# A decoder step on one core: the sample's requests ordered behind a power on POOL, a buffer of its own for the attention's queries, and the softmax factor of the cross-attention on ScalarE

## The chip, the cores and the metric

The kernel runs on one core of a Trainium2 chip. A core has TensorE (matmul; PE in the profile, with PEld for its weight loads), VectorE (DVE), ScalarE (ACT), GpSimd (POOL) and SyncE (SP). DMA requests are issued from queues: here SP asks for the weights and for most of the prompt's data, ACT for some stores, and POOL for everything large that the sample needs. Each of these engines works through its own list of instructions in order, so a request that waits for a free buffer holds up what stands behind it on the same engine. The metric is the time of one execution on the device in microseconds, here the median of several runs.

## The reference

One step of a decoder layer for two groups of rows that share the weights: a prompt of 1024 rows, and a sample of 8 requests with one new row each and 8192 cached positions behind it. Cut to what matters:

```python
# per group: x is (1, 1024, 1024) for the prompt and (8, 1, 1024) for the sample
q, k, v, logf, u, z = mixer_inputs(rmsnorm(x, g_mix), w_in, b_f, g_sgu_v)
att = fox_prompt(q, k, v, logf)          # causal, 8 heads of 64, with a forget term
#   or fox_sample(...)                   # against 64 pages of 128 cached keys and values per request
x = x + concat(rmsnorm(att), rmsnorm(sgu(u, z))) @ w_o
x = x + cross_attend(rmsnorm(x, g_cross), mk, mv, w_cq, w_co)   # 4 heads of 256, 256 memory rows
h = rmsnorm(x, g_ffn) @ w_up             # 2 x 2816 columns, then a causal convolution of width 3
x = x + (silu(gate) * val) @ w_down
y = rmsnorm(x, g_final)

def cross_attend(xn, mk, mv, w_cq, w_co):
    q = xn @ w_cq
    s = einsum('bqhd,bmhd->bhqm', q, mk) * 256 ** -0.5
    return einsum('bhqm,bmhd->bqhd', softmax(s), mv) @ w_co
```

Besides the two results, the new keys, values, forget terms, memory keys and values and the last rows of the convolution are returned.

## The kernel before

**Prompt.** Each large matmul is made of three: both operands are split into a rounded part and a rest (`split`: ScalarE writes the rounded part, VectorE the rest), and `gemm3` adds the three products that count. Weights come in pieces of 128 x 1024 through `wraw` and `wload` (L247, split at L233 and L234). The 1024 rows go through in two halves. `p1` makes the input projection; its last columns are done for four row tiles at once by `by_rows`. Then come `attention(0)`, `attention(1)`, and for each half the merge, the output projection, the cross-attention `cross`, and the gated MLP `ffn`.

**Attention.** It works on four pairs of heads. For each pair `load` fetches queries (L693), keys (L699) and values (L700), and `setup`, a generator of two steps, prepares the operands: the first step transposes the queries (L710) and splits them (L717, L734), the second does the same with the keys (L739, L744, L748). Then `scores` makes the maxima (L773, L776) and the exponentials (L774, L777), `turn` transposes them (L796) and `values` multiplies by the values (L812). The queries' tile comes from `T2`, a ring of seven buffers which also holds the exponentials of the first half, evictions on their way to memory (L680, for example) and other rows. The load and the first step of pair 0 are asked for inside `p1` by `early`, just before the last `by_rows`.

**Cross-attention.** For each head, `weigh` takes the row maxima of the raw scores, two row tiles at a time (L1137, VectorE), multiplies them by the factor of the row, `rq` (L1138, VectorE), and passes them as bias to the exponentials (L1141, ScalarE), which use `rq` as scale:

```python
nc.vector.tensor_reduce(mx[:, g2], sv, axis=AX.X, op=ALU.max, negate=True)
nc.vector.tensor_tensor(mx[:, g2], mx[:, g2], rq[:, g2], op=ALU.mult)
```

**Sample.** Its work is a background generator, `sample`, mixed into the prompt's at a pace given by hand (`PACE`). `decode` reads the cached keys and values of the 8 requests, 1 MB at a time, into four buffers (`KV`). VectorE multiplies and adds for the keys (L1384, L1388), PE for the values (L1444). Then `sample_rest` takes the 8 rows through the layer: `sample_proj` with `w_o`, a norm, `sample_proj` with `w_cq` (L1548 requests, L284 multiplies, L1538 adds up), the memory keys and values, `w_co`, a norm, `w_up` (L1700, L1709) and `w_down` (L1745, L1754). All these pages go through the same four buffers, and their requests stand on POOL. The norm `rms8` squares on ScalarE (L228), adds (L1520), and `rstd_of` scales (L221, VectorE) and raises to the power -1/2 on POOL (L222). The rows are then scaled (L1528) and transposed (L309). Between the second norm and `w_up`, the state of the convolution is read into one of the four buffers and a part of it stored again from there (L1691, to the output `o_s1`).

**Order.** The program is written in the order of these generators. A planner then lays out each engine's list when the program is built: of what could start, by its own estimate of durations, it takes what was written first. `tc.issue_after(ins)` orders the instructions of a block behind `ins` on the engine of `ins`; it adds no wait between engines.

Of the kernel before, what the change touches and what calls it, by code (L numbers as in the profile page):

```python
# [7 lines left out]
F32 = mybir.dt.float32  # L8
# [10 lines left out]
P = 128  # L19
D = 1024  # L20
# [58 lines left out]
def build(nc, tc, ctx, a, phases=None):  # L79
# [38 lines left out]
        return t  # L118

    def T2(n=512, dt=F32):  # L120
        return tpool.tile([P, 520], dt, tag="t2", bufs=NT, name=nm("t2"))[:, :n]

    def KV():
        return dpool.tile([P, 2048], F32, tag="kv", bufs=NKV, name=nm("kv"))
# [99 lines left out]

    def ssq_into(dst, src):
        n = src.shape[-1]
        j = tpool.tile([P, 1024], BF16, tag="junk", bufs=1, name=nm("junk"))[: src.shape[0], :n]
        nc.scalar.activation(j, src, AF.Square, accum_out=dst)  # L228

    def split(src, h, l, scale=None):  # L230
# [455 lines left out]
    def attention(hf, late=None, at=3):  # L686
# [2 lines left out]

        def load(hp):  # L690
            cs = slice(hp * P, (hp + 1) * P)
            qn = T2().rearrange("p (i c) -> p i c", c=P)
            nc.sync.dma_start(qn, q_d[hf * 512 : (hf + 1) * 512, cs].rearrange("(i p) c -> p i c", p=P))  # L693
            if hf == 0:
                kvn = U([P, 2 * nk, P])
                kn, vn = kvn[:, :nk, :], kvn[:, nk:, :]
            else:
                kn, vn = T2().rearrange("p (i c) -> p i c", c=P), U([P, nk, P])
            nc.sync.dma_start(kn, k_d[hf * 512 : nk * P, cs].rearrange("(i p) c -> p i c", p=P))  # L699
            nc.sync.dma_start(vn, v_d[: nk * P, cs].rearrange("(i p) c -> p i c", p=P))  # L700
            return qn, kn, vn
# [144 lines left out]

        got = []
        first = setup(0, *load(0))
        next(first)
        yield 2  # L850
        for _ in first:
            pass
        nxt = None
# [232 lines left out]
    def cross(xt, sq):  # L1086
# [37 lines left out]

        def weigh(h):
            mx = sm([P, 4], "cmx", 2)
            pp[h] = U([P, 4, 256])
            l4 = sm([P, 4], "cl", 2)
            r4 = sm([P, 4], "cr", 2)
            for g in range(2):  # L1130
                sv = BK().rearrange("p (i m) -> p i m", m=256)
                for i2 in range(2):
                    i = g * 2 + i2
                    for dd in range(2):
                        mmul(sv[:, i2, :], q2[h][:, dd, i * P : (i + 1) * P], mkT[h][:, dd, :], start=(dd == 0), stop=(dd == 1))
                g2 = slice(g * 2, g * 2 + 2)
                nc.vector.tensor_reduce(mx[:, g2], sv, axis=AX.X, op=ALU.max, negate=True)  # L1137
                nc.vector.tensor_tensor(mx[:, g2], mx[:, g2], rq[:, g2], op=ALU.mult)  # L1138
                for i2 in range(2):
                    i = g * 2 + i2  # L1140
                    nc.scalar.activation(  # L1141
                        pp[h][:, i, :], sv[:, i2, :], AF.Exp, bias=mx[:, i : i + 1], scale=rq[:, i : i + 1], accum_out=l4[:, i : i + 1]
                    )
            nc.vector.reciprocal(r4, l4)
            for i in range(4):
                nc.scalar.activation(pp[h][:, i, :], pp[h][:, i, :], AF.Copy, scale=r4[:, i : i + 1])
# [364 lines left out]
            yield left  # L1511


    def rms8(src):

        ss = sm([8, 2], "ss2", 1)
        for n in range(2):
            ssq_into(ss[:, n : n + 1], src[n])
        st = sm([8, 1], "sss", 1)
        nc.vector.tensor_tensor(st, ss[:, 0:1], ss[:, 1:2], op=ALU.add)  # L1520
        return rstd_of(st, D, 1, "r1")

    def sample_norm(src, gain, dst):
        r = rms8(src)
# [16 lines left out]
    def sample_proj(w, xT, fin):  # L1541
        outs = []
        for n in range(2):
            ps = (DV, MS)[n]()
            for kk in range(4):
                if kk % 2 == 0:
                    raw = KV().rearrange("p (k n) -> p k n", n=512)
                    nc.gpsimd.dma_start(raw, w[kk * 256 : (kk + 2) * 256, n * 512 : (n + 1) * 512].rearrange("(k p) n -> p k n", p=P))  # L1548
                    yield 1
                sample_mm(ps, raw[:, (kk % 2) * 2 : (kk % 2) * 2 + 2, :], kk, xT, 512)  # L1550
            outs.append(sample_out(n, ps, fin))
            next(outs[n])
        for o in outs:
            yield from o
        yield 1

    def sample_rest(xs):
# [46 lines left out]
        for b in range(8):  # L1604
            qb = [D2(), D2()]
            for n in range(2):
                nc.gpsimd.dma_start(qb[n], q2s_d[b : b + 1, n * 512 : (n + 1) * 512].broadcast_to((P, 512)))
            kv = KV()
            nc.gpsimd.dma_start(kv.rearrange("p (a c) -> p a c", c=D), a["cmk"][b].rearrange("(a p) c -> p a c", p=P))
            kvv = kv.rearrange("p (a c) -> p a c", c=D)  # L1610
            with behind(ENG.DVE):
                for n in range(2):
                    kn = kvv[:, :, n * 512 : (n + 1) * 512]
                    nc.vector.tensor_tensor(kn, kn, qb[n].unsqueeze(1).broadcast_to((P, 2, 512)), op=ALU.mult)
                for i in range(2):
                    nc.vector.tensor_reduce(sS[:, i, b, :], kvv[:, i, :].rearrange("p (h d) -> p h d", h=4), axis=AX.X, op=ALU.add)
            yield CMK
# [24 lines left out]
        for b0 in range(0, 8, 2):  # L1642
            kvs = []
            for b in (b0, b0 + 1):
                kvs.append(KV().rearrange("p (a c) -> p a c", c=D))
                nc.gpsimd.dma_start(kvs[-1], a["cmv"][b].rearrange("(a p) c -> p a c", p=P))

            for b in (b0 + 1, b0):
                with tc.issue_after(newest(ENG.PE)) if b == b0 else nullcontext():
                    for n in range(2):  # L1650
                        for mt in range(2):
                            j = n * 2 + mt
                            mmul(
                                po[32 * j : 32 * j + 32, :],
                                pz[:, mt, b, :],
                                kvs[b - b0][:, mt, n * 512 : (n + 1) * 512],
                                start=(b == 1),
                                stop=(b == 6),
                                tile_position=(0, 32 * j),
                            )  # L1660
            yield 2
# [33 lines left out]
        for f4 in range(11):  # L1695
            ps, rvs = DV(), []
            for q in range(2):
                raw = KV()
                f = f4 * 4 + q * 2
                nc.gpsimd.dma_start(raw.rearrange("p (f d) -> p f d", f=2), a["w_up"][f : f + 2].rearrange("f p d -> p f d"))  # L1700
                rvs.append(raw.rearrange("p (f k c) -> p k f c", f=2, c=P))
            if folds:
                folds.pop()()
# [37 lines left out]
        for f4 in range(0, NF, 4):  # L1741
            raws = []
            for f2 in range(f4, min(f4 + 4, NF), 2):
                raws.append(KV().rearrange("p (f d) -> p f d", f=2))
                nc.gpsimd.dma_start(raws[-1], a["w_down"][f2 * P : (f2 + 2) * P, :].rearrange("(f p) d -> p f d", p=P))  # L1745
            yield 1
            behind_ = None
            for n in range(2):
# [236 lines left out]
```

## Time and profile before

| | |
|---|---|
| median of 3 runs | 1862.74 us (1859.68 to 1864.82) |
| profiled execution | 1866.47 us |
| its span | 1864.6 us |
| mean granted TensorE clock | 0.98 |
| DMA moved | 521.27 MB, mean 280 GB/s |

A line of the timeline gives start, length, engine, line of the code, operation, output and input, and in brackets how long the engine was idle before it and what ended that wait. A line of the waits names who waited for whom, then the total, the number of times and the longest. A line of the windows gives a stretch and in it the busy time of PE, PEld, DVE, ACT and POOL with the number of instructions, then the granted TensorE clock (1.00 is full), the busy share of the DMA engines and GB/s. A line of a group has the number of instructions after x, then busy time, the mean of one in ns, and the idle time before them.

### The profile page before, as it was taken

The page shows a single profiled execution, that of the slowest core. Times are in us where ns is not written, and L with a number is a line of the kernel's source. Part 1 is how long each engine was busy: PE and PEld are TensorE (multiplying, and loading weights), DVE is VectorE, ACT ScalarE, POOL GpSimd, SP SyncE. Part 2 cuts the span into 40 slices and gives each one's busy share as a digit, 9 for nine tenths or more (in the row PEclk, how much of TensorE's full clock was granted, in tenths as well). Part 3 has the DMA queues.
Part 4 walks back from the last instruction along what each step waited for, and adds up shares of the span by engine and source line. Part 5 has one row for each costly group of instructions (what it writes and reads, how often), then busy time and mean ns, then how long its engine had stood idle before and what let it go on. Part 6 is the DMA issues. An engine that isn't in the chain of part 4 may idle for free.

```text
span 1864.6 us, 24289 instructions
## 1 busy us (share of the span) xinstructions
PE 1787.5 (96%) x9239; PEld 1299.2 (70%) x9239; DVE 1398.8 (75%) x1736; ACT 735.8 (39%) x1341; POOL 499.3 (27%) x461
## 2 busy tenths in 40 slices
PE   8999999888998999999999999998999999999998
PEld 5887676556676667767777776766676668767765
DVE  4788667888778787989989899898874559644344
ACT  6332364466633535323333234234353333232332
POOL 1243323433142322223242223234322111101110
PEclk9999999899999999999999999999999999999999
DMA  8877886967687975878878789988869577767971
GB/s 316 290 267 265 312 276 239 298 231 230 238 345 287 346 289 209 309 249 328 304 279 319 260 305 344 355 311 329 304 241 349 203 291 259 264 205 260 356 263 59
DMA packets 157012, 521.27 MB, mean 280 GB/s; under 512 B 20808, under 2 KB 40520, under 8 KB 124128
## 3 DMA queue, kind: packets, MB, share of 16 engines
q0 software_dynamic: 57168, 341.14, 49.0%
q1 hardware_dynamic: 92816, 165.99, 25.8%
q10 hardware_dynamic: 6912, 12.59, 1.8%
q8 instruction: 73, 1.20, 0.3%
q14 instruction: 43, 0.35, 0.1%
HBM read 495.73 MB, written 23.93 MB: 279 GB/s over the span
## 4 chain that ended last, share of the span: by engine, by line
PE 59%; DMA 7%; DVE 5%; issue 4%; ACT 2%; POOL 1%; DVEq 0%; POOLq 0%; ACTq 0%
PE ba L270 8%; PE ba L272 8%; PE ba L271 8%; PE bb L270 4%; PE bb L271 4%; PE bb L272 4%; PE dv L1444 4%; DMA kv<-cache_v,kidx 2%; DMA kv<-cache_k,kidx 2%; DVE s L1388 1%; DVE kv L1384 1%; PE dv L1709 1%; PE ba L1021 1%; DMA u<-an_d 1%; PE bb L812 1%
## 5 line engine op out<-in xcount | busy, mean ns | idle before, releaser
L233 ACT ACTIVATE wh<-wr 128x1024 fp32r<-128x1024 f32 (+2 forms) x220 | 228.8, 1044 | 516.6 <-PE ba L271 192.0
L234 DVE TENSOR_TENSOR wl<-wr,wh 128x1024 fp32r<-128x1024 f32 (+2 forms) x220 | 262.9, 1201 | 144.6 <-PE ba L272 62.4
L1368 POOL DMA_INDIRECT kv<-cache_k,kidx x128 | 194.8, 1522 | 569.5 <-DVE s L1388 317.4
L1384 DVE TENSOR_TENSOR kv<-kv,d 128x1024 f32<-128x1024 f32 (+1 forms) x156 | 258.0, 1681 | 29.8 <-DMA kv<-cache_k,kidx 29.5
L1388 DVE TENSOR_REDUCE s<-kv 128x16 f32<-128x1024 f32 (+1 forms) x156 | 258.0, 1673 | 0.0
L1438 POOL DMA_INDIRECT kv<-cache_v,kidx x128 | 159.2, 1244 | 314.7 <-PE dv L1444 244.4
L270 PE MATMUL ba<-u,wh 128*128 128x512 f32 (+1 forms) x560 | 221.3, 397 | 2.0 <-ACT u L236 1.9
L271 PE MATMUL ba<-u,wh 128*128 128x512 f32 (+1 forms) x560 | 221.1, 395 | 1.3 <-DVE u L237 1.2
L272 PE MATMUL ba<-u,wl 128*128 128x512 f32 (+1 forms) x560 | 220.5, 395 | 0.0
L270 PE MATMUL ba<-wh,u 128*128 128x512 f32 (+1 forms) x495 | 187.5, 381 | 0.0
L271 PE MATMUL ba<-wl,u 128*128 128x512 f32 (+1 forms) x495 | 186.5, 378 | 0.0
L272 PE MATMUL ba<-wh,u 128*128 128x512 f32 (+1 forms) x495 | 184.0, 377 | 0.0
L1444 PE MATMUL dv<-kv,s 128*32 128x512 f32 x1024 | 128.1, 603 | 5.0 <-DMA kv<-cache_v,kidx 3.0
L270 PEld LDWEIGHTS ba<-u,wh 128*128 128x128 f32 x560 | 107.0, 191 | 34.6 <-issue 7.2
L272 PEld LDWEIGHTS ba<-u,wl 128*128 128x128 f32 x560 | 107.1, 191 | 32.9 <-issue 9.2
L271 PEld LDWEIGHTS ba<-u,wh 128*128 128x128 f32 x560 | 107.1, 191 | 30.9 <-issue 6.3
L271 PE MATMUL bb<-u,wh 128*128 128x512 f32 (+1 forms) x304 | 118.3, 390 | 8.7 <-DVE u L237 8.7
L270 PE MATMUL bb<-u,wh 128*128 128x512 f32 (+1 forms) x304 | 117.8, 388 | 0.2 <-ACT u L236 0.2
L272 PE MATMUL bb<-u,wl 128*128 128x512 f32 (+1 forms) x304 | 117.1, 386 | 0.0
L270 PEld LDWEIGHTS ba<-wh,u 128*128 128x128 f32 x495 | 93.8, 190 | 27.0 <-issue 8.0
L271 PEld LDWEIGHTS ba<-wl,u 128*128 128x128 f32 x495 | 93.7, 189 | 20.7 <-issue 4.2
L272 PEld LDWEIGHTS ba<-wh,u 128*128 128x128 f32 x495 | 93.5, 189 | 19.7 <-issue 2.5
(437 smaller groups left out, 3293.7 us busy)
## 6 DMA issues: line engine op xcount, KB each, us to landing
wr<-w_up SPq DMA_DIRECT2D x88, 512.0 KB
kv<-w_up POOLq DMA_DIRECT2D x22, 1024.0 KB
wr<-w_down SPq DMA_DIRECT2D x40, 512.0 KB
kv<-w_down POOLq DMA_DIRECT2D x11, 1024.0 KB
wr<-w_in SPq DMA_DIRECT2D x16, 512.0 KB
wr<-w_o SPq DMA_DIRECT2D x16, 512.0 KB
wr<-w_cq SPq DMA_DIRECT2D x16, 512.0 KB
wr<-w_co SPq DMA_DIRECT2D x16, 512.0 KB
```

Source lines behind the costliest of these rows:

```text
L233: nc.scalar.activation(h, src, AF.Copy)
L234: nc.vector.tensor_tensor(l, src, h.bitcast(F32), op=ALU.subtract)
L270: mmul(out, sh, mh, start=(i == 0), stop=False)
L271: mmul(out, sh, ml, start=False, stop=False)
L272: mmul(out, sl, mh, start=False, stop=(i == n - 1))
L812: mmul(po[64 * j : 64 * j + 64, q0:256], vn[:, kt, 64 * j : 64 * j + 64], pt[j][kt // 4][:, kt % 4, q0:256], start=(kt == 0), stop=(kt == ...
L1021: mmul(pss[i], mh[k][:, tb], wh, start=(k == korder[0]), stop=False)
L1368: nc.gpsimd.indirect_dma_start(kv, None, a["cache_k"], off(kidx[:, b, ch : ch + 1]))
L1384: nc.vector.tensor_tensor(kvv[:, i : i + m, :], kvv[:, i : i + m, :], qb.unsqueeze(1).broadcast_to((P, m, 512)), op=ALU.mult)
L1388: nc.vector.tensor_reduce(s[:, ch * 4 + i : ch * 4 + i + m, :].rearrange("p k h -> p (k h)"), kvv[:, i : i + m, :].rearrange("p k (h d) -> ...
L1438: nc.gpsimd.indirect_dma_start(kv, None, a["cache_v"], off(kidx[:, b, ch : ch + 1]))
L1444: mmul(dv[32 * j : 32 * j + 32, :], s[:, ch * 4 : ch * 4 + 4, :].rearrange("p k h -> p (k h)"), kvv[:, j, :], start=(ch == 1), stop=(ch == ...
```

## The change

It has four parts.

- `page` issues the sample's large requests behind the newest power that `rms8` put on POOL. Before the first `rms8`, and so for `w_o`, nothing is ordered.
- The attention's queries have a tile of their own, `qn`, with one buffer, in place of one of the seven of `T2`.
- In the first half both steps of the first `setup` are asked for in one go inside `p1`.
- In `weigh` the product with `rq` becomes two ScalarE copies with `rq` as scale, into a small tile of its own, `cbs`.

To make room, the tiles of `T2` go from 520 to 512 columns, and `ssq_into` writes the squares of rows over 512 wide over their source instead of into a buffer of 1024.

```diff
     def T2(n=512, dt=F32):
-        return tpool.tile([P, 520], dt, tag="t2", bufs=NT, name=nm("t2"))[:, :n]
+        return tpool.tile([P, 512], dt, tag="t2", bufs=NT, name=nm("t2"))[:, :n]
...
     def ssq_into(dst, src):
         n = src.shape[-1]
-        j = tpool.tile([P, 1024], BF16, tag="junk", bufs=1, name=nm("junk"))[: src.shape[0], :n]
+
+        j = src if n > 512 else tpool.tile([P, 512], BF16, tag="junk", bufs=1, name=nm("junk"))[: src.shape[0], :n]
         nc.scalar.activation(j, src, AF.Square, accum_out=dst)
...
         def load(hp):
             cs = slice(hp * P, (hp + 1) * P)
-            qn = T2().rearrange("p (i c) -> p i c", c=P)
+            qn = tpool.tile([P, 512], F32, tag="qn", bufs=1, name=nm("qn")).rearrange("p (i c) -> p i c", c=P)
...
         first = setup(0, *load(0))
-        next(first)
-        yield 2
+        if hf:
+            next(first)
+            yield 2
         for _ in first:
             pass
...
         def weigh(h):
             mx = sm([P, 4], "cmx", 2)
+            bs = sm([P, 4], "cbs", 2)
...
-                nc.vector.tensor_tensor(mx[:, g2], mx[:, g2], rq[:, g2], op=ALU.mult)
+                for i2 in range(2):
+                    i = g * 2 + i2
+                    nc.scalar.activation(bs[:, i : i + 1], mx[:, i : i + 1], AF.Copy, scale=rq[:, i : i + 1])
                 for i2 in range(2):
                     i = g * 2 + i2
                     nc.scalar.activation(
-                        pp[h][:, i, :], sv[:, i2, :], AF.Exp, bias=mx[:, i : i + 1], scale=rq[:, i : i + 1], accum_out=l4[:, i : i + 1]
+                        pp[h][:, i, :], sv[:, i2, :], AF.Exp, bias=bs[:, i : i + 1], scale=rq[:, i : i + 1], accum_out=l4[:, i : i + 1]
                     )
...
+    rows8 = []
+
+    def page(dst, src):
+
+        with tc.issue_after(rows8[0]) if rows8 else nullcontext():
+            nc.gpsimd.dma_start(dst, src)
+
     def rms8(src):
...
-        return rstd_of(st, D, 1, "r1")
+        r = rstd_of(st, D, 1, "r1")
+        rows8[:] = [newest(ENG.Pool)]
+        return r
...
-                    nc.gpsimd.dma_start(raw, w[kk * 256 : (kk + 2) * 256, n * 512 : (n + 1) * 512].rearrange("(k p) n -> p k n", p=P))
+                    page(raw, w[kk * 256 : (kk + 2) * 256, n * 512 : (n + 1) * 512].rearrange("(k p) n -> p k n", p=P))
...
-                nc.gpsimd.dma_start(raw.rearrange("p (f d) -> p f d", f=2), a["w_up"][f : f + 2].rearrange("f p d -> p f d"))
+                page(raw.rearrange("p (f d) -> p f d", f=2), a["w_up"][f : f + 2].rearrange("f p d -> p f d"))
```

The other four requests of `sample_rest` (the rows of the query, the memory keys and values, `w_down`) are changed to `page` in the same way.

More of the change, by code (lines that the diff above doesn't have):

```diff
@@ L1606, in sample_rest @@
             for n in range(2):
-                nc.gpsimd.dma_start(qb[n], q2s_d[b : b + 1, n * 512 : (n + 1) * 512].broadcast_to((P, 512)))
+                page(qb[n], q2s_d[b : b + 1, n * 512 : (n + 1) * 512].broadcast_to((P, 512)))
             kv = KV()
-            nc.gpsimd.dma_start(kv.rearrange("p (a c) -> p a c", c=D), a["cmk"][b].rearrange("(a p) c -> p a c", p=P))
+            page(kv.rearrange("p (a c) -> p a c", c=D), a["cmk"][b].rearrange("(a p) c -> p a c", p=P))
             kvv = kv.rearrange("p (a c) -> p a c", c=D)
@@ L1645, in sample_rest @@
                 kvs.append(KV().rearrange("p (a c) -> p a c", c=D))
-                nc.gpsimd.dma_start(kvs[-1], a["cmv"][b].rearrange("(a p) c -> p a c", p=P))
+                page(kvs[-1], a["cmv"][b].rearrange("(a p) c -> p a c", p=P))
             for b in (b0 + 1, b0):
@@ L1744, in sample_rest @@
                 raws.append(KV().rearrange("p (f d) -> p f d", f=2))
-                nc.gpsimd.dma_start(raws[-1], a["w_down"][f2 * P : (f2 + 2) * P, :].rearrange("(f p) d -> p f d", p=P))
+                page(raws[-1], a["w_down"][f2 * P : (f2 + 2) * P, :].rearrange("(f p) d -> p f d", p=P))
             yield 1
```

## The prediction

> **What bounds the kernel now.** I read the busy totals first, then what each engine waits for, then stretches of a few microseconds where TensorE waits, with the timeline of the engines in them.
>
> ```profile
> span 1864.6 us, 24289 instructions
> PE 1787.5 (96%) x9239; PEld 1299.2 (70%) x9239; DVE 1398.8 (75%) x1736; ACT 735.8 (39%) x1341; POOL 499.3 (27%) x461
> ```
>
> TensorE stands still for 1864.6 - 1787.5 = 77.1 us; everything else that an edit can win must make its work shorter or its clock higher. No part of the diff removes matmuls. So the question is which of those idle microseconds the diff touches, and what each does to the clock. The next rows are one idle stretch, in the columns span, busy PE, PEld, DVE, ACT, POOL, then granted clock, DMA share and GB/s.
>
> ```profile
> 1676.00:1680.00 4.00, 1.04 (x9) 1.02 (x9) 1.57 (x3) 0.00 (x0) 1.26 (x2) 0.83 0.33 73
> 1680.00:1684.00 4.00, 4.00 (x10) 3.13 (x11) 3.37 (x8) 1.29 (x2) 0.00 (x0) 0.50 0.81 321
> 1684.00:1688.00 4.00, 4.00 (x28) 2.84 (x30) 2.68 (x5) 1.64 (x4) 0.00 (x0) 0.81 0.35 121
> ...
> 1284.00:1288.00 4.00, 1.67 (x17) 1.39 (x19) 4.00 (x5) 2.70 (x8) 3.10 (x1) 1.00 0.99 365
> 1288.00:1292.00 4.00, 4.00 (x27) 2.32 (x20) 2.89 (x4) 1.08 (x3) 2.50 (x2) 1.00 1.01 376
> ```
>
> A stall costs more than itself: after the one at 1676 PE is "busy" for 8 us, but at clocks of 0.50 and 0.81, which loses 4 x 0.50 + 4 x 0.19 = 2.8 us of work. A stall that leaves 4.00 - 1.67 = 2.3 us open (1284 to 1288) leaves the clock at 1.00.
>
> **Part 1: the sample's requests behind the power on POOL (`page`).** `rms8` ends in a power on POOL, L222. The diff orders every later request of the sample behind the newest such power. In most places that is already the order; two differ.
>
> ```profile
> 1661.87 14.66 DMA o_s<-kv
> ...
> 1659.64 0.70 POOL L1700 DMA_DIRECT2D kv<-w_up  x1 [25.00 <-PE dv L284]
> ...
> 1677.11 0.71 POOL L1700 DMA_DIRECT2D kv<-w_up  x1 [15.03 <-DMA o_s<-kv]
> 1677.84 0.55 POOL L222 TENSOR_TENSOR r1r<-r1r,mhalf 8x1 f32<-8x1 f32 x1
> ...
> 1669.71 0.14 DVE L221 TENSOR_SCALAR r1r<-sss 8x1 f32<-8x1 f32 x1
> 1678.43 0.87 DVE L1528 TENSOR_SCALAR s<-dec,r1r 8x512 f32<-8x512 f32 x2 [8.58 <-POOL r1r L222]
> ...
> 1678.96 1.02 PE L309 MATMUL ms<-cp,s 8*128 8x8 f32 x8 [3.19 <-DVE s L1528]
> 1687.26 1.93 PE L1709 MATMUL dv<-kv,xsT 128*32 128x256 f32 x32
> ```
>
> The last norm's input is ready at 1669.85, but its power waits on POOL's queue behind the fourth request for `w_up`, which waits for a KV buffer that the store of `o_s1` holds for 14.66 us. VectorE waits 8.58 us for the power and PE 3.19 us for VectorE. With the power first that wait is gone: **3.2 us of stall and 2.8 us of clock, 6.0 us**. Late next are the requests themselves: the first goes out at about 1670.4 instead of 1659.64, the fourth still at 1677. The transposes L309 come 8 us sooner, the first matmuls L1709 wait for the pages. Bounds: 6.0 at best; nothing, or a little less than nothing, if PE stands before L1709 instead (rivals).
>
> The other place is `w_cq`.
>
> ```profile
> 1488.79 2.46 POOL L1548 DMA_DIRECT2D kv<-w_cq  x3 [11.49 <-PE dv L284]
> ...
> 1499.93 0.56 POOL L222 TENSOR_TENSOR r1r<-r1r,mhalf 8x1 f32<-8x1 f32 x1 [5.73 <-DVE r1r L221]
> ...
> 1511.36 1.92 PE L284 MATMUL dv<-kv,xsT 128*32 128x512 f32 x16
> 1513.10 1.90 PE L284 MATMUL ms<-kv,xsT 128*32 128x512 f32 x16
> ...
> 1488.00:1506.00 18.00, 18.00 (x91) 10.81 (x80) 6.81 (x12) 4.86 (x9) 3.59 (x5) 1.00 0.86 312
> 1496.00:1500.00 4.00, 4.00 (x16) 2.34 (x15) 0.97 (x3) 1.35 (x4) 0.07 (x1) 1.00 0.99 393
> 1508.00:1512.00 4.00, 4.00 (x23) 2.73 (x25) 1.92 (x2) 1.06 (x1) 0.00 (x0) 1.00 0.01 3
> ```
>
> Four requests of 1024 KB (`sample_proj` makes two for each half; three stand in the first row) now start before the power and would start after it, at 1500.5: 11.7 us later. Before, they streamed in the 18 us from 1488 to 1506; by 1508 the DMA engines are empty. Those 18 us moved 312 x 18 = 5.6 MB, 4.2 of it these pages, so other loads took some 80 GB/s. From 1500.5 the first two pages need 8.6 us (half of the 17.2 from 1488.8 to 1506) and land at 1509, ahead of 1511.36. All four need 17.2 us at that pace (1517.7, 4.6 us after 1513.10), or at the 393 GB/s of the row of 1496 less 80 GB/s 13.4 us (1513.9, 0.8 late). I take the second, since that row has the queue full, which it will be: **0.8 us lost**. Bounds: nothing, and 4.6 + 2.8 of clock = 7.4.
> The Trainium skill ("DMA: Bandwidth & Descriptors", section "Anatomy of one DMA — SWDGE (gpsimd) path") gives 2.0 us plus bytes over 436 GB/s. By that estimate four pages need 11.6 us, land at 1512.1, and this term would be nothing; the 18 us of the row speak against it.
>
> **Part 2: the factor in `weigh` goes to ScalarE.** Sixteen VectorE products become 32 ScalarE copies of one column.
>
> ```profile
> L1138 DVE TENSOR_TENSOR cmx<-cmx,rq x16: 118/150/176, 618.7 to 1308.7; 128x2 f32<-128x2 f32 x16
> L989 ACT ACTIVATE fac<-sqx,part x8: 282/293/297, 702.8 to 1380.0; 128x1 f32<-128x1 f32 x8
> L1248 ACT ACTIVATE hlast<-ba 128x2 f32<-128x2 f32 x61 | 9.8, 160 | 0.0
> ...
> 1297.59 1.28 DVE L1137 TENSOR_REDUCE cmx<-ba 128x2 f32<-128x512 f32 x2
> 1298.79 2.33 DVE L1388 TENSOR_REDUCE s<-kv 128x16 f32<-128x1024 f32 x2
> 1301.05 0.22 DVE L1138 TENSOR_TENSOR cmx<-cmx,rq 128x2 f32<-128x2 f32 x2
> ...
> 1301.23 0.56 ACT L1141 ACTIVATE u<-ba,cmx,rq 128x256 f32<-128x256 f32 x1 [3.32 <-DVE cmx L1138]
> ...
> 1302.48 3.13 PE L1135 MATMUL ba<-t,u 128*128 128x256 f32 x8 [3.86 <-ACT u L1141]
> 1304.00:1308.00 4.00, 4.00 (x13) 3.15 (x13) 3.72 (x7) 3.05 (x8) 1.28 (x2) 0.67 0.76 244
> ...
> 649.60 3.72 PE L1135 MATMUL ba<-t,u 128*128 128x256 f32 x16 [1.03 <-ACT t L1123]
> ```
>
> VectorE is relieved of 16 x 0.15 = 2.4 us. A copy lies between 0.16 us (no factor from a tile) and 0.29 us (a factor, alone in its queue); I take 0.2 in a run of several, so 0.4 us per pair and 6.4 us of ScalarE in all, with 5.1 and 9.4 as ends. The copies wait for the maxima where the exponentials waited for the product, so the same work stands behind them on ScalarE. At 1297 the maxima are done at 1298.87, then two reductions of the sample (2.33 us) cut in before the product. The copies start at 1298.9, the exponentials at 1299.3 instead of 1301.23, and PE's 3.86 us stall shrinks by 1.9 us; what is left, 2.0 us, is shorter than the 2.3 us that did not lower the clock, so the 0.33 x 4 = 1.3 us lost from 1304 come back too: 3.2 us. Against it, where PE waits for a ScalarE that is never free, as at 649.60, four copies ahead come to 0.8 us; I count two such places, 1.6. **Net 1.6 us won**; bounds 3.2 won, and 6.4 lost if ScalarE's queue is the path everywhere.
> The skill's page "TensorE: Matmul & The Clock Gate" (section "HAM oscillation — how this bites in real kernels") asks for no PE-idle gaps over about 3.4 us. By that rule the 3.19 us stall of part 1 should have left the clock alone, that term would be 3.2, and the whole sum 5.6 instead of 8.4; the 0.50 from 1680 to 1684 contradicts it, so I keep the rows.
>
> **Part 3: a buffer for the queries, and the first operands in one step.**
>
> ```profile
> SPq L693 <- DMA o_mv<-t: 21.1, 2, 12.1
> SPq L693 <- PE ms L812: 8.8, 1, 8.8
> ...
> 249.07 0.38 SPq L699 DMA_DIRECT2D u<-o_k  x1
> ...
> 276.11 0.50 SPq L693 DMA_DIRECT2D t<-q_d  x1
> ...
> 261.39 0.60 PE L739 MATMUL ba<-cp,u 128*128 128x128 f32 x4
> ...
> 277.01 0.33 PE L796 MATMUL bb<-cp,t 128*128 128x128 f32 x1 [2.36 <-ACT t L774]
> ...
> 282.05 1.11 PE L710 MATMUL ba<-cp,t 128*128 128x128 f32 x4 [1.58 <-DMA t<-q_d]
> ...
> 330.00:512.00 182.00, 156.40 (x1031) 108.26 (x1030) 152.76 (x273) 103.64 (x234) 57.04 (x75) 0.92 0.74 247
> ```
>
> The loads of the queries (L693) wait three times on SP, 29.9 us together, for a slot of the ring that also holds evictions on their way to memory. With a buffer of its own the load waits only for the previous pair's transposes, long done. PE is seen to pay 1.58 us for that, at 282: I count **1.6 us**. I leave the clock out there, since the 2.36 us stall ahead of it stays. Behind these loads on SP stand keys, values and weights, so up to a quarter of what PE loses from 330 to 512 (25.6 us idle and 0.08 x 156 = 12.5 us of clock), 10 us, is the upper end. The k-transposes of pair 0 move ahead of the last matmuls of p1. Their keys are requested at 249.07, and if they take the 5.9 us that the queries took from 276.11 to 282.05, they land at 255. They run at 261.39 now; ordered too early they could hold PE for 3.5 us and cost 2.8 of clock, the lower end. I cost this edit at nothing: `by_rows` hides it until its last matmul at 261.
>
> The narrower ring and the squares written in place change no instruction's shape on the path, only what is written: nothing.
>
> **The sum**: 6.0 - 0.8 + 1.6 + 1.6 = 8.4 us. The profiled execution took 1866.47 us (span 1864.6 and 1.87 around it), so it would take 1858.1. The median of the three runs is 1862.74, 0.2% lower; from there **1854.3 us**.
>
> **Rivals.**
> *A, the stalls move.* The program's order on each engine is planned when it is built, and each edit shifts it; PE then waits a few microseconds for something else, and the gains of parts 1 and 3 are spent. Or the load of the queries stays late because the weights ahead of it on SP do. For it: DVE is busy 152.76 of 182 us in the attention, so the next wait is near. Against: the stall at 1676 has one cause and it is removed. Part 2's 1.6 is left: about 1861.
> *B, the pages come too late: slower.* PE reaches the sample's matmuls before the delayed requests land. At 1513.10 that costs 7.4 us. Part 1 brings L309 and with it L1709 8.0 us forward, from 1687.26 to 1679.3. The pages for it go out at 1670.4; two need 8.6 us at the pace of `w_cq`, and 3.0 more if the store of `o_s1`, which ends at 1676.5, takes half of the DMA engines until then: 1682.0, a wait of 2.7 us and 2.8 of clock, so part 1 shrinks from 6.0 to 0.5. With nothing from parts 2 and 3 that is 6.9 us lost: 1869.6. The point from which it decides: the two waits with their clock outweigh what the parts still bring. Against it: PE has the prompt's matmuls to put there if the order expects the delay.
> *C, SP is freed for real.* Part 3 brings its 10 us: 8.4 + 8.4 = 16.8, 1846.
>
> **Chances.** Forecast 0.45, A 0.28, B 0.15, C 0.12. This kernel can tell about 0.3% (5.6 us) from no change, so faster means under 1857.1 and slower over 1868.3. Of the forecast 0.42 lies under that line; with C faster 0.54. A and 0.03 are within: 0.31. Slower 0.15. The range takes in C's middle with 3 us below it and most of B: 1843 to 1870. The likeliest sign alone (forecast and C) spans 1843 to 1857.
>
> **What would show it.** On POOL, L222 directly behind its L221 near 1670 and no stall over 1 us at L309; clock 1.00 from 1680 to 1688. L284's second half for `w_cq` with a wait under 1 us; a wait over 4 us there, or at L1709, is B. ScalarE's copies right behind the maxima, PE's stall near 1302 at 2 us. No wait of L693 on SP for evictions. The 1854 falls if the idle total of PE does not drop from 77 to about 71 us.

## The result, and the profile after

The changed kernel takes **1848.36 us** (median of 6 runs, 1845.14 to 1854.37) where the kernel before took 1864.07 (6 runs): a ratio of 0.9917, 95% interval 0.99 to 0.9934. That is 15.7 us by the medians and 17.9 us between the two profiled executions (1866.47 and 1848.6). The forecast was 8.4 us and 1854.3; the time lies in its range of 1843 to 1870, and the gain is nearly twice what the sum gave. So the question behind this result is where the other half came from. One of the twelve executions of `two_tiles`, an experiment below, took 2493.54 us at a mean granted clock of 0.653 for a reason that nothing here shows, and its ratio leaves that execution out.

The busy totals of the profile after:

```profile
span 1846.8 us, 24292 instructions
PE 1776.3 (96%) x9239; PEld 1288.6 (70%) x9239; DVE 1395.2 (76%) x1720; ACT 743.1 (40%) x1373; POOL 491.9 (27%) x461
```

TensorE now stands still for 1846.8 - 1776.3 = 70.5 us, 6.6 less than before. Its busy time fell by 1787.5 - 1776.3 = 11.2 us with the same 9239 matmuls. A busy time that shrinks with equal work is a higher clock: most of the gain is clock, not idle time.

The windows of the kernel after, at the times of the prediction's (columns as there: span, busy PE, PEld, DVE, ACT, POOL, granted clock, DMA share, GB/s):

```profile
1676.00:1680.00 4.00, 4.00 (x42) 2.46 (x41) 2.47 (x5) 2.38 (x4) 1.41 (x2) 1.00 0.84 316
1680.00:1684.00 4.00, 4.00 (x21) 3.30 (x19) 0.06 (x1) 0.63 (x1) 0.00 (x0) 1.00 0.78 230
1684.00:1688.00 4.00, 4.00 (x45) 2.82 (x45) 0.70 (x1) 1.33 (x2) 1.41 (x2) 1.00 0.89 334
...
1304.00:1308.00 4.00, 4.00 (x15) 2.04 (x15) 4.00 (x4) 2.88 (x7) 1.45 (x2) 1.00 0.93 340
330.00:512.00 182.00, 155.91 (x1046) 106.75 (x1045) 151.45 (x274) 107.19 (x240) 55.05 (x72) 0.94 0.73 247
```

The dips at 1680 (0.50) and 1304 (0.67) are gone. Since the changed kernel is some 12 us ahead by then, the same work stands earlier in it; there is no dip there either, as the table of the stages below shows. In the attention (330 to 512) PE is as busy as before, at 0.94 instead of 0.92.

POOL's part of the timeline after, first at `w_cq`, then at `w_up`:

```profile
1487.68 0.54 POOL L222 TENSOR_TENSOR r1r<-r1r,mhalf 8x1 f32<-8x1 f32 x1 [22.62 <-DVE r1r L221]
1488.18 2.45 POOL L1524 DMA_DIRECT2D kv<-w_cq  x3
1492.07 0.75 POOL L1524 DMA_DIRECT2D kv<-w_cq  x1 [1.45 <-PE ba L273]
...
1662.95 0.88 POOL L222 TENSOR_TENSOR r1r<-r1r,mhalf 8x1 f32<-8x1 f32 x1 [36.26 <-DVE r1r L221]
1663.79 2.89 POOL L1524 DMA_DIRECT2D kv<-w_up  x4
```

Both powers stand ahead of their requests. At `w_up` four requests follow in 2.89 us, where before the last one and the power sat behind a wait of 15.03 us. At `w_cq` the norm came 12 us sooner than before (L222 at 1487.68, then 1499.93), since the kernel is that far ahead by then, so the requests go out at the same time as before.

SP's waits for the load of the queries, after (total, times, longest):

```profile
SPq L694 <- PE ba L711: 69.9, 7, 19.3
...
SPq L694 <- DMA qn<-q_d: 5.6, 1, 5.6
```

This speaks against the prediction's reason for part 3. The load no longer waits for evictions, but for the transposes that still read the one buffer, and far longer: 69.9 us instead of 29.9.

### The profile page after: what moved, and what is told of

It reads as the page before. It is cut to its first block, busy times and chain, and to the rows that moved or that the text cites. A ratio compares the mean times of both kernels' runs of the same rounds, so it can differ in the third digit from the quotient of the medians.

```text
span 1846.8 us, 24292 instructions
## 1 busy us (share of the span) xinstructions
PE 1776.3 (96%) x9239; PEld 1288.6 (70%) x9239; DVE 1395.2 (76%) x1720; ACT 743.1 (40%) x1373; POOL 491.9 (27%) x461
## 3 DMA queue, kind: packets, MB, share of 16 engines
q1 hardware_dynamic: 92816, 165.99, 25.7%
## 4 chain that ended last, share of the span: by engine, by line
PE 76%; DMA 7%; issue 6%; DVE 6%; ACT 3%; POOL 1%; SPq 0%; POOLq 0%; DVEq 0%; ACTq 0%
PE ba L273 10%; PE ba L271 10%; PE ba L272 10%; PE bb L273 5%; PE bb L271 5%; PE bb L272 5%; PE dv L1449 5%; DMA kv<-cache_v,kidx 2%; DMA kv<-cache_k,kidx 2%; PE ba L1023 1%; PE ba L1025 1%; PE ba L1024 1%; PE dv L1723 1%; DMA u<-an_d 1%; PE ba L1043 1%
## 5 line engine op out<-in xcount | busy, mean ns | idle before, releaser
L1373 POOL DMA_INDIRECT kv<-cache_k,kidx x128 | 169.5, 1325 | 580.0 <-DVE s L1393 328.9
L1443 POOL DMA_INDIRECT kv<-cache_v,kidx x128 | 173.3, 1354 | 303.0 <-PE dv L1449 246.3
```

The costliest lines, as they stand in the source:

```text
L1373: nc.gpsimd.indirect_dma_start(kv, None, a["cache_k"], off(kidx[:, b, ch : ch + 1]))
L1443: nc.gpsimd.indirect_dma_start(kv, None, a["cache_v"], off(kidx[:, b, ch : ch + 1]))
```

## The experiments

Twelve kernels: each part alone, the whole without each part, and then the queries' part taken to pieces. Every ratio is to the kernel before on the same chip.

| kernel | median us | before, us | ratio | 95% interval |
|---|---|---|---|---|
| the changed kernel, first comparison | 1848.36 | 1864.07 | 0.9917 | 0.99 to 0.9934 |
| only_page | 1862.01 | 1864.81 | 0.998 | 0.9965 to 0.9996 |
| only_weigh | 1868.23 | 1864.81 | 1.0013 | 0.9997 to 1.0028 |
| only_queries | 1863.44 | 1864.81 | 0.9989 | 0.9973 to 1.0006 |
| only_room | 1863.97 | 1864.81 | 0.9987 | 0.9968 to 1.0007 |
| whole_again | 1849.55 | 1866.21 | 0.9904 | 0.989 to 0.9919 |
| without_page | 1853.65 | 1866.21 | 0.9929 | 0.9915 to 0.9944 |
| without_weigh | 1855.66 | 1866.21 | 0.9942 | 0.9922 to 0.9962 |
| without_queries | 1863.54 | 1866.21 | 0.9989 | 0.9975 to 1.0003 |
| without_step | 1848.67 | 1864.81 | 0.9914 | 0.9894 to 0.9935 |
| without_tile | 1861.53 | 1864.81 | 0.9985 | 0.9969 to 1.0 |
| two_tiles | 1854.74 | 1864.81 | 0.9952 | 0.9933 to 0.9971 |
| both_halves | 1857.19 | 1864.81 | 0.9955 | 0.9939 to 0.9972 |

### Each part alone

`only_page` has the part `page` of the diff and nothing else:

```diff
-                nc.gpsimd.dma_start(raw.rearrange("p (f d) -> p f d", f=2), a["w_up"][f : f + 2].rearrange("f p d -> p f d"))
+                page(raw.rearrange("p (f d) -> p f d", f=2), a["w_up"][f : f + 2].rearrange("f p d -> p f d"))
```

> Only the sample's requests go behind the power; the lists of all engines are those of before up to about 1480 us. Theory (each part pays where its lines run): the stall of 3.19 us before L309 and the clock after it go, 5 us won, about 1859, all of it after 1640. Rival (the gain of the change comes from the new order that the queries' buffer causes everywhere): within 2 us of before, because the transposes come sooner but the pages do not, and PE waits before the w_up matmuls instead.

Ratio 0.998. Windows of `only_page` and, for comparison, of the kernel before:

```profile
1640.00:1700.00 60.00, 60.00 (x325) 41.48 (x324) 33.43 (x56) 24.56 (x42) 6.19 (x9) 1.00 0.65 220
```

```profile
1640.00:1700.00 60.00, 56.81 (x301) 39.56 (x301) 31.06 (x51) 21.03 (x37) 6.27 (x9) 0.94 0.61 188
```

The 3.19 us of idle time and the clock are both won back, with nothing lost before the matmuls of `w_up`. The interval (0.7 to 6.5 us of 1864.81) holds the 5 us expected and also a part of the rival's "within 2 us"; the window shows the mechanism.

`only_weigh` has the copies in `weigh`:

```diff
-                nc.vector.tensor_tensor(mx[:, g2], mx[:, g2], rq[:, g2], op=ALU.mult)
+                for i2 in range(2):
+                    i = g * 2 + i2
+                    nc.scalar.activation(bs[:, i : i + 1], mx[:, i : i + 1], AF.Copy, scale=rq[:, i : i + 1])
```

> Only the factor in weigh goes to ScalarE; the order changes in the two cross-attentions (about 610 to 680 and 1260 to 1310) and shortly around them. Theory: the stall of 3.86 us at 1302 shrinks and its clock comes back, 2 to 5 us won, 1859 to 1862, nearly all in the second cross-attention. Rival: not over 1 us won (1863 to 1866), since the 5.5 us that the changed kernel gained between 1186 and 1375 came from the shifted order of the sample's work and not from the factor.

Ratio 1.0013: alone it wins nothing. The theory of 2 to 5 us fell, though the stall it was aimed at went: from 1255 to 1335 PE's one wait over 1 us is 2.51 us for a load of the sample, and the 3.86 us for the exponentials are gone.

`only_queries` has the queries' tile, the one step, and the room for them:

```diff
-            qn = T2().rearrange("p (i c) -> p i c", c=P)
+            qn = tpool.tile([P, 512], F32, tag="qn", bufs=1, name=nm("qn")).rearrange("p (i c) -> p i c", c=P)
...
-        next(first)
-        yield 2
+        if hf:
+            next(first)
+            yield 2
```

> The queries' tile, one step at the first setup, and the room for it; this changes the order of the lists from 4% of the way on, to the end. Theory: 1.6 us in the attention, and then 3 to 5 us between 720 and 1260 by other stalls, where the changed kernel gained 5.0 without an edited line there: 1858 to 1862. Rival 1 (only the attention counts): 1862 to 1864. Rival 2 (the shift is luck and falls out otherwise without the two other parts): slower than before by up to 5 us.

Ratio 0.9989, interval across 1. Rival 1 is nearest.

`only_room` has the ring of 512 columns and the squares in place:

```diff
-        return tpool.tile([P, 520], dt, tag="t2", bufs=NT, name=nm("t2"))[:, :n]
+        return tpool.tile([P, 512], dt, tag="t2", bufs=NT, name=nm("t2"))[:, :n]
...
-        j = tpool.tile([P, 1024], BF16, tag="junk", bufs=1, name=nm("junk"))[: src.shape[0], :n]
+        j = src if n > 512 else tpool.tile([P, 512], BF16, tag="junk", bufs=1, name=nm("junk"))[: src.shape[0], :n]
```

> Only the ring of 512 columns and the squares written in place; the lists of PE, DVE, POOL and SP stay as they were, ScalarE's has a few rows in another place in the first tenth. Theory: within 1 us of before. Rival: the squares in place wait for readers of their source, which costs over 2 us.

Ratio 0.9987, not distinguishable from 1. It also shows how far two executions of the same order lie apart. Its lists of PE, DVE, POOL and SP are those of before, and yet, in the window of the attention:

```profile
330.00:512.00 182.00, 158.86 (x1022) 109.84 (x1023) 151.03 (x269) 102.40 (x231) 55.54 (x74) 0.89 0.71 243
```

The clock is 0.89 where the profiled execution of before had 0.92, a difference of some 0.03 x 157 = 4.7 us in one stage (6.9 by the finer windows of the table below). One execution of each kernel can't settle a question of this size.

The single ratios leave 0.2%, -0.13% and 0.11%, together 0.2% where the whole change brings 0.8 to 1%. The parts don't add up by their medians.

### The whole without a part

`whole_again` is the changed kernel once more.

> The changed kernel once more, beside the three that leave a part out. If its first comparison holds, 12 to 19 us under before (ratio 0.990 to 0.9935).

Ratio 0.9904: the gain is there again, 16.7 us.

`without_page` has the plain requests again:

```diff
-                page(raw.rearrange("p (f d) -> p f d", f=2), a["w_up"][f : f + 2].rearrange("f p d -> p f d"))
+                nc.gpsimd.dma_start(raw.rearrange("p (f d) -> p f d", f=2), a["w_up"][f : f + 2].rearrange("f p d -> p f d"))
```

> The changed kernel without the ordering of the sample's requests. Theory (the power ahead of the requests for w_up is worth 6 us wherever the rest stands): 4 to 7 us over the changed kernel, 7 to 12 under before. Rival (in the new order the power would have come in time anyway): within 2 us of the changed kernel.

Ratio 0.9929, 4.1 us over `whole_again`: the theory's lower end. The old stall is back, in POOL's and PE's timeline of this kernel:

```profile
1666.63 0.72 POOL L1705 DMA_DIRECT2D kv<-w_up  x1 [15.32 <-DMA o_s<-kv]
1667.37 0.56 POOL L222 TENSOR_TENSOR r1r<-r1r,mhalf 8x1 f32<-8x1 f32 x1
```

```profile
1668.50 1.02 PE L310 MATMUL ms<-cp,s 8*128 8x8 f32 x8 [3.47 <-DVE s L1533]
```

`without_weigh` has the product on VectorE again:

```diff
-                for i2 in range(2):
-                    i = g * 2 + i2
-                    nc.scalar.activation(bs[:, i : i + 1], mx[:, i : i + 1], AF.Copy, scale=rq[:, i : i + 1])
+                nc.vector.tensor_tensor(mx[:, g2], mx[:, g2], rq[:, g2], op=ALU.mult)
```

> The changed kernel with the product of weigh back on VectorE. Alone the factor on ScalarE won nothing (ratio 1.0013). Theory (it pays in the order that the queries' buffer makes, by the stall in the second cross-attention): 4 to 7 us over the changed kernel. Rival (it is worth nothing here either, and the rest of the gain is that of page and the queries): within 2 us of the changed kernel, or under it.

Ratio 0.9942, 6.1 us over `whole_again`: here the factor on ScalarE does pay. The second cross-attention in `without_weigh`, then in `whole_again`:

```profile
1260.00:1325.00 65.00, 60.23 (x270) 38.98 (x270) 56.30 (x72) 34.40 (x76) 23.57 (x17) 0.97 0.81 311
```

```profile
1260.00:1325.00 65.00, 62.95 (x294) 39.73 (x289) 59.23 (x67) 37.99 (x94) 24.72 (x19) 1.00 0.83 318
```

Idle time and clock together: 4.77 + 60.23 x 0.03 = 6.6 us against 2.05.

`without_queries` is `page` and `weigh` alone; the attention is that of before.

```diff
-            qn = tpool.tile([P, 512], F32, tag="qn", bufs=1, name=nm("qn")).rearrange("p (i c) -> p i c", c=P)
+            qn = T2().rearrange("p (i c) -> p i c", c=P)
...
-        if hf:
-            next(first)
-            yield 2
+        next(first)
+        yield 2
```

> The sample's requests and the factor in weigh alone, the attention as before. If parts add up, the ratios of the single parts give 0.998 x 1.0013 = 0.999, 2 us under before. Theory (the queries' buffer and the one step shift the order to one in which the other two parts pay): 1860 to 1865, 12 to 16 us over the changed kernel. Rival (page and weigh help each other, as both clear the sample's work from ScalarE, VectorE and POOL in the second half): 1850 to 1856.

Ratio 0.9989: 14.0 us over `whole_again`. The theory holds against the rival. Its profiled execution was the fastest of its twelve, 5.8 us under the median, so its row in the table of the stages flatters it. The queries' part, which alone shows no gain, is worth most of the change once the other two are there.

### Which piece of the queries' part

At this point I believed in the one step, since it brings work forward, and not in the tile, whose wait on SP had grown.

`without_step`:

```diff
-        if hf:
-            next(first)
-            yield 2
+        next(first)
+        yield 2
```

> The changed kernel with the first setup in two steps again; the queries keep their tile. Five executions in the old order lost 12.9 us of clock on the mean from 330 to 512, five in the new order 5.4. Theory (the one step makes the new order, the tile does not): back to an order like the old one, 10 us and more of clock lost from 330 to 512, 1857 to 1864. Rival (the tile makes it): within 3 us of the changed kernel, 1847 to 1853.

Ratio 0.9914, as fast as the whole. The theory fell: the step is worth nothing that can be seen.

`without_tile`:

```diff
-            qn = tpool.tile([P, 512], F32, tag="qn", bufs=1, name=nm("qn")).rearrange("p (i c) -> p i c", c=P)
+            qn = T2().rearrange("p (i c) -> p i c", c=P)
```

> The changed kernel with the queries in the ring of seven again; the first setup stays one step. From 40% to 60% of the lists the order is that of the changed kernel, only the first 40% and the second cross-attention differ. Theory (the step counts): 1847 to 1854, 3 to 7 us of clock lost from 330 to 512, though SP waits for evictions again. Rival (the prediction's: the tile frees SP of 29.9 us of waits): 1856 to 1862, with a wait for q_d on PE.

Ratio 0.9985: without the tile nearly all the gain is gone, 15 us by the ratios of this kernel and of `whole_again`. The middle of the lists, from 40% to 60%, is the changed kernel's, so this comes from ahead of the 40%, where the attention lies, or from behind the 60%. The window of the attention, first in `without_step`, then in `without_tile`:

```profile
330.00:512.00 182.00, 156.12 (x1058) 107.48 (x1057) 156.20 (x278) 106.79 (x238) 56.68 (x72) 0.95 0.75 257
```

```profile
330.00:512.00 182.00, 155.22 (x1004) 106.58 (x1004) 148.11 (x268) 102.08 (x231) 61.80 (x80) 0.92 0.72 240
```

PE is idle for 25.9 and 26.8 us, nearly the same. The clock differs, and with it what got done: 1058 matmuls recorded against 1004 in this stretch.

`two_tiles` asks whether the new wait of SP costs anything:

```diff
-NT = 7
+NT = 6
...
-            qn = tpool.tile([P, 512], F32, tag="qn", bufs=1, name=nm("qn")).rearrange("p (i c) -> p i c", c=P)
+            qn = tpool.tile([P, 512], F32, tag="qn", bufs=2, name=nm("qn")).rearrange("p (i c) -> p i c", c=P)
```

> The changed kernel with two buffers for the queries and six in place of seven in the ring. In the changed kernel SP stands 69.9 us before the queries' load, waiting for the transposes that read the one buffer; here that wait goes, and up to 36% of the list PE's order is the same. Theory (SP's wait is hidden): within 3 us of the changed kernel, 1846 to 1853. Rival (SP is late for all behind that load): 4 us and more faster, under 1845.

Ratio 0.9952, slower than the whole and, with a median of 1854.74, 1.7 us over the upper end of what the theory expected and far from the rival's. It did not do what it was built for:

```profile
SPq L694 <- PE ba L711: 53.6, 5, 20.3
...
SPq L694 <- PE ba L772: 6.3, 1, 6.3
```

SP still waits 53.6 us for the transposes, and its loads start no earlier than in the kernel after (277.44, 321.53 and 356.23 against 275.64, 319.09 and 355.12); why is not shown. That SP's wait is hidden is therefore not shown either. Only this is: six buffers in the ring and two for the queries are no better than seven and one.

`both_halves`:

```diff
         first = setup(0, *load(0))
-        if hf:
-            next(first)
-            yield 2
         for _ in first:
             pass
         nxt = None
+        if hf:
+            yield 2
         yield 2
```

> The changed kernel with the first setup in one step in the second half as well; the order changes from 21% to 40% of PE's list and in the second cross-attention. Theory (what the step brought in the first half was an order in which stalls fall apart, and not work brought forward): no gain to be counted on, 1847 to 1856. Rival (asking for the operands earlier is a gain by itself): 2 to 5 us faster, 1843 to 1847.

Ratio 0.9955, about 8 us slower than the whole and just past the upper end of what was expected; asking earlier is no gain by itself.

### Where the time lies, stage by stage

For every profiled execution I took the windows of 4 us that lie wholly inside a stage and summed what PE lost: idle time, and busy time x (1 - granted clock). The three stages in which the kernels differ, in us; "ring" and "own" say where the queries lie, and for the attention proper (330 to 512) idle and clock stand apart.

| kernel | queries | 330 to 512: idle, clock | 240 to 600, both | 1260 to 1440, both | 1640 to 1700, both |
|---|---|---|---|---|---|
| before | ring | 25.3, 9.9 | 49.9 | 11.7 | 6.1 |
| only_page | ring | 27.9, 9.7 | 53.1 | 12.0 | 0.0 |
| only_weigh | ring | 22.9, 16.2 | 56.2 | 7.7 | 4.7 |
| only_room | ring | 23.2, 16.8 | 52.3 | 12.2 | 2.8 |
| without_queries | ring | 25.7, 12.0 | 51.4 | 9.2 | 0.0 |
| without_tile | ring | 26.8, 10.2 | 56.9 | 4.4 | 0.0 |
| after | own | 26.1, 6.6 | 46.8 | 3.9 | 0.0 |
| whole_again | own | 25.6, 4.3 | 47.4 | 3.6 | 0.0 |
| without_page | own | 25.0, 3.7 | 45.0 | 4.0 | 6.4 |
| without_weigh | own | 25.8, 3.8 | 47.5 | 7.6 | 0.0 |
| only_queries | own | 24.2, 8.5 | 50.7 | 7.8 | 4.6 |
| without_step | own | 25.9, 5.2 | 44.1 | 6.1 | 0.0 |
| two_tiles | own | 25.8, 3.5 | 46.4 | 6.0 | 0.0 |
| both_halves | own | 23.6, 9.2 | 49.3 | 5.3 | 0.0 |

From 600 to 1260 all of them lose 19 to 24 us, without a pattern. The rest reads as follows.

- **Attention.** Six executions with the queries in the ring lose 25.3 us of idle time and 12.5 us of clock on the mean from 330 to 512; eight with a tile of their own 25.3 and 5.6. The idle time is the same; 6.9 us of clock are not. From 240 to 600 the means are 53.3 and 47.2: 6.1 us. These are not fourteen orders: up to 600, five of the six in the ring have the order of before (`without_tile` is the sixth), and six of the eight others that of after (all but `without_step` and `both_halves`). The two kinds nearly meet, at 9.7 us of clock (`only_page`) and 9.2 (`both_halves`).
- **Second cross-attention.** With product and ring 12.0 on the mean of three, with the copies alone 8.5 (only_weigh, without_queries), with the own tile alone 7.7, with both 3.8 (after, whole_again, without_page). Both parts pay there, about 4 us each, in idle time as well as in clock (8.8 and 2.8 us before, 4.0 and nothing after). In the second of these the tile is not what counts most: without it 4.4 are lost, without the step 6.1. The other two orders with both parts lose 6.0 (two_tiles) and 5.3 (both_halves).
- **Tail.** 4.9 on the mean of five without `page`, nothing in nine with it.

By these means 6.1 + (12.0 - 3.8) + 4.9 = 19.2 us, against 15.7 and 16.7 measured. By the rows of before and after alone it is 3.1 + 7.8 + 6.1 = 17.0, of the 17.9 us between these two executions: there the second cross-attention gives the largest share and the attention the smallest. The timed executions, which list their mean granted clock, say the same of the tile: 0.9886 on the mean of `whole_again`, 0.9873 in `without_step`, 0.9828 in `without_tile`, 0.9816 in the kernel before. (0.9886 - 0.9828) x 1850 us is 10.7 us, of the 12.0 by which the medians of `whole_again` and `without_tile` differ (an estimate: the clock as a share of the whole span).

That equal idle time can cost different clocks is seen in the windows of the attention, first in the kernel before, then in `whole_again`:

```profile
388.00:392.00 4.00, 2.39 (x14) 1.85 (x16) 4.00 (x7) 2.51 (x5) 0.00 (x0) 0.98 1.00 388
392.00:396.00 4.00, 2.53 (x14) 1.22 (x10) 3.62 (x5) 1.82 (x5) 0.00 (x0) 0.59 0.69 171
396.00:400.00 4.00, 2.92 (x17) 2.09 (x18) 3.32 (x9) 2.80 (x9) 0.58 (x1) 0.83 0.08 26
440.00:444.00 4.00, 1.28 (x4) 0.96 (x4) 3.01 (x4) 2.16 (x4) 0.94 (x1) 0.88 1.00 361
444.00:448.00 4.00, 4.00 (x26) 3.54 (x25) 2.79 (x4) 2.36 (x7) 0.00 (x0) 0.69 0.94 371
```

```profile
364.00:368.00 4.00, 4.00 (x24) 3.82 (x22) 3.97 (x11) 2.31 (x7) 3.66 (x6) 0.57 0.98 292
368.00:372.00 4.00, 0.71 (x5) 0.47 (x4) 3.91 (x9) 1.91 (x6) 2.48 (x4) 0.89 0.92 245
372.00:376.00 4.00, 0.38 (x1) 0.08 (x1) 4.00 (x9) 0.00 (x0) 0.00 (x0) 0.50 0.71 258
376.00:380.00 4.00, 3.27 (x17) 1.74 (x17) 0.50 (x3) 0.45 (x3) 0.52 (x1) 0.50 0.61 227
...
388.00:404.00 16.00, 14.10 (x104) 9.71 (x98) 13.77 (x25) 12.28 (x31) 5.54 (x7) 1.00 0.67 232
440.00:444.00 4.00, 2.42 (x14) 1.66 (x13) 3.93 (x8) 1.20 (x2) 2.33 (x3) 1.00 0.74 246
444.00:448.00 4.00, 3.17 (x26) 2.55 (x25) 3.96 (x7) 3.56 (x7) 0.00 (x0) 1.00 1.05 383
```

In `whole_again` 6.9 us of idle time lie in one place, from 368 to 376, where PE works for only 1.1 us, so a clock of 0.50 there costs little. That saves nothing on the whole, for the windows on both sides of it run at 0.57 and 0.50: from 332 to 384 the kernel before loses 4.6 us of clock and `whole_again` 4.3. All of the difference lies from 384 to 512. There the kernel before has 14.2 us of idle time and loses 5.3 us of clock; `whole_again` has 12.5 us and loses none.

What differs behind 384 is the size of the portions. In the kernel before 2.72 us are idle from 440 to 444, and the next 4 us run at 0.69. In `whole_again` no window of 4 us there has more than 1.60 us idle, and all of them run at 1.00. The same holds of the other kernels: the five that lose no clock from 384 to 512 (after, whole_again, without_page, without_weigh, two_tiles) have at most 1.61 us idle in a window, and the six with the queries in the ring have a window with 1.8 to 3.0 us and lose 3.9 to 9.0 us. `both_halves`, with its own tile, has one with 2.6 us and loses 5.1; `without_step` lies between, with 1.74 and 1.4. This is no sharp line. In the kernel before 1.61 us (388 to 392) were followed by 0.59; `only_queries` lost 3.3 us with at most 1.58 us in a window; and 2.3 us, at 1284 in the kernel before, left 1.00. That large portions are the cause is read from these traces; no experiment moved one stall by itself.

## Why the prediction was right, and where it was wrong

- **Idle from 77 to about 71 us**: 70.5. **Faster**: yes. The size: 15.7 instead of 8.4. The range, from 20 us faster to 7 slower, held nearly every rival too, so that the time lies in it says little for the mechanism; the parts below say more.
- **Part 1, 6.0 at `w_up`**: right in mechanism and size. The profiled executions show 6.1 gone, five executions without `page` lose 4.9 on the mean, the ratios of `only_page` and `without_page` give 3.7 and 4.7 us. The rule of the Trainium skill ("TensorE: Matmul & The Clock Gate", section "HAM oscillation — how this bites in real kernels") that was weighed there would have left the clock out and made it 3.2; the 60 us from 1640 to 1700, 3.2 idle and 2.9 of clock before and neither after, decide for the rows. The power stands behind its L221 as forecast; it came at 1662.95 instead of near 1670 because everything ahead was earlier.
- **Part 1, 0.8 lost at `w_cq`, and rival B**: the delay happened, the loss did not. Without `page` in the changed kernel POOL asks for these pages ahead of the power, from 1475.17 on (first fence, POOL's timeline of `without_page`); with it they go out 13 us later, at 1488.18, and the matmuls start at nearly the same time (second fence, PE's timeline after; 1497.74 in `without_page`). In both kernels, and in the one before, the first of them starts 11.4 us behind the start of the power:

```profile
1475.17 2.46 POOL L1553 DMA_DIRECT2D kv<-w_cq  x3 [11.47 <-PE dv L285]
...
1486.32 0.56 POOL L222 TENSOR_TENSOR r1r<-r1r,mhalf 8x1 f32<-8x1 f32 x1 [5.73 <-DVE r1r L221]
```

```profile
1499.11 1.06 PE L285 MATMUL dv<-kv,xsT 128*32 128x512 f32 x8
1501.46 1.06 PE L285 MATMUL dv<-kv,xsT 128*32 128x512 f32 x8
1504.73 1.06 PE L285 MATMUL ms<-kv,xsT 128*32 128x512 f32 x8
```

No wait stands behind them. The planner cut them into halves, one for each page, and between these PE does the prompt's work, so that the last of them ends near 1509.7 (near 1501.4 in `without_page`) without a wait. That is what the prediction had named as the reason against B.

- **Part 2, net 1.6**: the 3.2 us in the second cross-attention are confirmed in kind and somewhat low in size: about 4 by the table. The stall of 3.86 us, forecast to shrink to 2.0, is gone, in the kernel after and with this part alone (`only_weigh`). The price of the copies was a little under-sized; ScalarE's group and its timeline after:

```profile
L1143 ACT ACTIVATE cbs<-cmx,rq x32: 278/288/298, 604.3 to 1301.3; 128x1 f32<-128x1 f32 x32
...
1299.18 0.48 ACT L1143 ACTIVATE cbs<-cmx,rq 128x1 f32<-128x1 f32 x2 [1.14 <-DVE cmx L1140]
```

A copy takes 288 ns, a pair 0.48 us instead of the 0.4 taken, so 16 pairs 7.7 us of ScalarE instead of 6.4. The loss of 1.6 us in the first half was not seen in the changed kernel (from 600 to 670, 3.6 us idle, 3.2 before). Alone the part wins nothing (1.0013), though it gains some 3.5 us in the second cross-attention there too. Its profiled execution lost 56.2 us from 240 to 600, against 49.9 before, ahead of its first edited line and in the same order of PE; whether this is chance, and where the gain goes in the other executions, isn't settled.
- **Part 3, 1.6**: this is the step that failed, in three ways. First, "the load waits only for the previous pair's transposes, long done": those transposes are not long done; SP waits longer than before, 69.9 us. Second, the wait of 1.58 us at 282 that the value was taken from is gone, but the kernel after has one of 1.43 us at a later pair:

```profile
365.77 1.12 PE L711 MATMUL ba<-cp,qn 128*128 128x128 f32 x4 [1.43 <-DMA qn<-q_d]
```

In `whole_again`, the same kernel, PE doesn't wait for the queries at all. Either way it is no more than 1.6 us. Third, "I leave the clock out there": in the attention the clock was, on the mean, the whole effect. Taking the tile out of the changed kernel costs 13 to 15 us (0.9985 against 0.9917 and 0.9904). By the table the attention gives 6.1 of them on the mean, with equal idle time, and 9.5 between `without_tile` and `whole_again`, 2.9 of them idle time. The sum also had nothing for the second cross-attention from this part, where the shifted order, some 700 us behind the edited lines, is worth about 4 us. The prediction's bound of 10 us, which counted a quarter of idle time and clock together, lies between what the attention shows and what the whole kernel loses without the tile.
- **The one step**: nothing, as forecast (0.9914 without it). **Ring and squares**: nothing, as forecast (0.9987, interval across 1).
- **Rival C** (1846) had the time almost exactly and the reason wrong: SP is not freed, so its number is luck. **Rival A** was right in that each edit moves stalls elsewhere, but they moved in the kernel's favour. That they did was no part of the forecast, and is luck too.

What stays open. The stage table adds up for the whole change, but its means would give `only_weigh` a gain of 3.5 us and `only_queries` one of 10, where the ratios show none that is clear of 1. Their own rows fit better: 0.9 us more lost than before, and 4.6 less. The misfit lies in the attention, where `only_queries` has the order of after up to 600 and still lost the most of its kind (50.7). So why the parts are worth so little alone and so much together is not shown. What the tile changes may be the order alone: `without_tile` has another order than the whole in the first 40%, and no run kept the order and took the tile away. `two_tiles`, which has the order of after up to 600 with other buffers, loses nearly the same there as the whole (46.4, then 46.8 and 47.4). Nor was it tried whether the tile acts as a place of its own or just as an eighth buffer beside the seven.

## What to carry to other kernels

Measure a part by taking it out of the whole as well as by putting it alone into the old kernel: here the queries' part showed 0.1% the one way and 0.9% the other. Where a planner lays out the order, read the granted clock of each stage beside its idle time, over several executions, before calling a stage unchanged. A gain with one visible cause (a power queued behind a request that waits) can be forecast to a microsecond or two (6.0 here, and 3.7 to 6.1 by the several ways of measuring it); the effect of one more buffer on an order can only be bounded, and its bound belongs in the forecast with the clock counted in.

## What the runs showed of the hardware that was not expected

- The clock lost is not a property of the order alone: with equal lists on PE, the profiled executions of the kernel before and of `only_room` lost 9.9 and 16.8 us of clock from 330 to 512. The Trainium skill ("TensorE: Matmul & The Clock Gate", section "What's actually happening") tells of an activity window of about 3.4 us that runs freely, so that the same kernel meets it at different points; these two numbers agree with that. It puts the fall of the clock behind a whole idle window; here 1.6 us of idle time from 388 to 392 in the kernel before were followed by 4 us at 0.59, and 1.6 us in `whole_again` (440 to 444) by 4 us at 1.00.
- The 3.19 us stall at 1679 halved the clock behind it in the profiled execution of before. In `only_room`, with the same order, the same place stalled for 1.3 us and still lost 1.5 of clock.
